# One k tile at a time: B of block 0 delivered in single k tiles between the row tiles of A, with 24 half-size staging slots

## The chip, the cores and the metric

The kernel runs on one core of one Trainium2 chip. The metric is the device time of one execution in microseconds (us). Executions of this kernel agree closely: 20 of the kernel before lie between 421.6 and 423.15 us. A difference of 1 us is therefore small but can be measured.

In the text PE is the matmul engine, DVE the vector engine, ACT the scalar engine, POOL the GpSimd engine and SP the sync engine. POOL and SP matter here mostly because they issue DMA transfers.

## The reference

```python
def setup_inputs():
    m, k, n = 1024, 4096, 4096
    return {"a": randn(m, k) as float32, "b": randn(k, n) as float32}   # shortened

def reference(a, b):
    x = np.matmul(a, b)
    return special.logsumexp(x, axis=-1).astype(np.float32)
```

A is 1024 x 4096, B is 4096 x 4096, and the output is one number for each of the 1024 rows.

## The kernel before

The kernel keeps A in SBUF as float16, transposed (`aT`), and goes through B in eight blocks of 512 columns. Blocks after the first use a scheme of sums and fewer products (its matmuls are on line 397 before and on line 416 after the change); it needs all of A transposed. This document is about the **opening**, in which A and block 0 of B arrive from HBM. Six of the eight row tiles of A are transposed by PE as they arrive, and their products with block 0 are done as plain matmuls in between.

A *round* of the opening is four k tiles (512 elements of k): six tiles of A, 128 x 512 each, and four k tiles of block 0 of B. There are eight rounds. A tile is 128 KB in float16, so a round writes 10 x 128 KB = 1.31 MB. POOL issues these transfers, because they cast float32 to float16 on the way. Only the first tile of A and the first two k tiles of B come as float32 from SP and are cast by DVE and ACT.

The order of arrivals, before. Two k tiles of B come in one transfer:

```python
    arrivals = []
    for k0 in range(0, KT, KN):            # KN = 4
        for m in range(MT - 2):            # six row tiles
            arrivals.append((k0, KN, "a", m))
            if m < KN // 2:
                arrivals.append((k0 + 2 * m, 2, "b", k0))
```

So a round is A0, B01, A1, B23, A2, A3, A4, A5: eight transfers. The work that follows an arrival, and the loading:

```python
    def behind(k0, kn, what, x):
        if what == "a":
            have_a.setdefault(k0, []).append(x)
            todo = [(k, x) for k in range(k0, k0 + kn) if k in have_b]
        else:
            have_b.update({k0: 1, k0 + 1: 1})
            todo = [(k, m) for k in (k0, k0 + 1) for m in have_a.get(x, [])]
        for k, m in todo:
            plain(acc[m // 2][m % 2], k // 2, k % 2, m)     # one 512-column matmul
        ...                                                 # (sums of A: cut)

    def first(k0, kn, what, x):
        ...                                                 # (A: cut, one SP transfer, DVE cast)
            raw = fix_pool.tile([P, 2, FD], f32, name="raw_b", tag="s")
            nc.sync.dma_start(out=raw, in_=b_rows[:, 0, :, 0:FD])
            nc.vector.tensor_copy(out=blk0.raw[0][:, 0, 0], in_=raw[:, 0])
            nc.scalar.copy(out=blk0.raw[0][:, 0, 1], in_=raw[:, 1])

    back = []
    for n, (k0, kn, what, x) in enumerate(arrivals):
        while coming and (coming[0][2] == "b" or loads[0] < count[0] + NSLOT):
            load(*coming.pop(0))            # POOL issues, as long as slots are free
            ...
        if what == "a":
            transpose_group(k0, kn, x)      # 4 PE transposes into PSUM, copy by DVE or ACT
        if k0 < KN and x < 3:
            warm(1)                         # a filler matmul
        if len(back) == 1 + (n >= MT) + (n >= 4 * MT):
            behind(*back.pop(0))            # matmuls lag the transposes by 1 to 3 arrivals
        back.append((k0, kn, what, x))
        while back and k0 < KN and what == "b":
            behind(*back.pop(0))
```

Of the kernel before, what the change touches and what calls it, by code (L numbers as in the profile page):

```python
# [13 lines left out]
def kernel(  # L14
# [6 lines left out]
    nc = tc.nc  # L21
    P = 128
    FD = 512
    H = FD // 2
    f32 = mybir.dt.float32
# [8 lines left out]
    MT, KT, NB = M // P, K // P, N // FD  # L34
    MP, KP = MT // 2, KT // 2
    G = 4
    GI = KP // G
    assert (MT, KT, NB) == (8, 32, 8)

    a_m = a.rearrange("(p mt) k -> mt p k", mt=MT)  # L40
    KN = 4
# [3 lines left out]
    fix_pool = ctx.enter_context(tc.tile_pool(name="fix", bufs=1))  # L45
# [12 lines left out]
            name=nc.get_next_instruction_name(),  # L58
# [8 lines left out]
    s2 = cst_pool.tile([P, KP, MP, P], f16, name="s2")  # L67
    s5 = cst_pool.tile([P, KP, MP, P], f16, name="s5")
    tb = cst_pool.tile([P, 3, KP, H], f16, name="tb")
    stg_slots = tb.rearrange("p t (i j) n -> p (t i) (j n)", j=4)  # L70
    NSLOT = 3 * KP // 4
    ident = cst_pool.tile([P, P], f16, name="ident")
    negmax = cst_pool.tile([P, MT, NB + 1], f32, name="negmax")
    tsum = cst_pool.tile([P, MT, NB + 1], f32, name="tsum")
# [50 lines left out]
    b_rows = b.rearrange("(i t p) n -> p i t n", p=P, t=2)  # L125

    class Block:
# [9 lines left out]
        def load(self, lo, hi):  # L137
            nc.gpsimd.dma_start(  # L138
                out=self.raw[lo // GI][:, lo % GI : lo % GI + hi - lo],
                in_=b_rows[:, lo:hi, :, ts(self.nb, FD)],  # L140
            )

        def load_all(self):
# [29 lines left out]
    blk0, blk1 = Block(0), Block(1)  # L173
# [13 lines left out]
    loads = [0]  # L187

    def load_a(k0, kn, m):
        slot = stg_slots[:, loads[0] % NSLOT, 0 : kn * P]  # L190
        loads[0] += 1
        nc.gpsimd.dma_start(out=slot, in_=a_m[m, :, k0 * P : (k0 + kn) * P])  # L192
        stg[k0, m] = slot

    count = [0]

    def transpose_group(k0, kn, m):
        src = stg.pop((k0, m))
        n = count[0]
        count[0] += 1  # L200
        pst = tps[n % 2]
        for j in range(kn):
            nc.tensor.matmul(  # L203
                pst[:, ts(j, P)],
                src[:, ts(j, P)],
                ident,
                is_transpose=True,
                start=(j == 0),
                stop=(j == kn - 1),
            )  # L210
        dst = aT[:, k0 // 2 : (k0 + kn) // 2, :, m // 2, m % 2, :]
        v = pst[:, 0 : kn * P].rearrange("p (i t c) -> p i t c", t=2, c=P)
        if n % 2 == 0:
            nc.vector.tensor_copy(out=dst, in_=v)  # L214
        else:
            nc.scalar.copy(out=dst, in_=v)  # L216
# [3 lines left out]
    def plain(pt, i, kp, m):  # L220
        nc.tensor.matmul(  # L221
            pt,
            aT[:, i, kp, m // 2, m % 2, :],
            blk0.raw[i // GI][:, i % GI, kp, :],
            start=(done[m] == 0),
            stop=(done[m] == KT - 1),
        )
        done[m] += 1

    def a_sums_early(r, q):  # L230
        a11, a12 = aT[:, r, 0, q, 0, :], aT[:, r, 1, q, 0, :]
        a21, a22 = aT[:, r, 0, q, 1, :], aT[:, r, 1, q, 1, :]
        add(s1[:, r, q], a11, a22)
        add(s2[:, r, q], a21, a22)
        add(s5[:, r, q], a11, a12)

    def a_sums_late(r, q):
        a11, a12 = aT[:, r, 0, q, 0, :], aT[:, r, 1, q, 0, :]
        a21, a22 = aT[:, r, 0, q, 1, :], aT[:, r, 1, q, 1, :]
        sub(a21, a21, a11)  # L240
        sub(a12, a12, a22)

    def first_max(m):
        lse_max(acc[m // 2][m % 2], m, 0)
        lse_exp(acc[m // 2][m % 2], m, 0)

    arrivals = []
    for k0 in range(0, KT, KN):
        for m in range(MT - 2):
            arrivals.append((k0, KN, "a", m))  # L250
            if m < KN // 2:
                arrivals.append((k0 + 2 * m, 2, "b", k0))
    in_place = []

    have_a, have_b = {}, {}

    def behind(k0, kn, what, x):
        if what == "a":
            have_a.setdefault(k0, []).append(x)
            todo = [(k, x) for k in range(k0, k0 + kn) if k in have_b]  # L260
        else:
            have_b.update({k0: 1, k0 + 1: 1})
            todo = [(k, m) for k in (k0, k0 + 1) for m in have_a.get(x, [])]
        for k, m in todo:
            plain(acc[m // 2][m % 2], k // 2, k % 2, m)
        r = slice(k0 // 2, (k0 + kn) // 2)
        if what == "a":
            if x >= 3 and in_place:
                a_sums_late(*in_place.pop(0))
            if x % 2 == 1 and k0 + kn < KT:  # L270
                a_sums_early(r, x // 2)
            if x == 5:
                in_place.extend([(r, 0), (r, 1), (r, 2)])
            if k0 + kn == KT and x == 4:
                first_max(0)
                first_max(1)
                for what in ("t1", "t6"):
                    blk1.make(what, 0, 2)

    def warm(n):  # L280
        for _ in range(n):
            nc.tensor.matmul(acc[2][1], zeros[:, 0:P], zeros[:, 0:FD], start=True, stop=True)  # L282

    zeros = s5[:, KP - 1].rearrange("p q c -> p (q c)")
    nc.vector.memset(zeros[:, 0:FD], 0.0)  # L285
    make_identity(nc, ident)
    nc.vector.memset(negmax, 3.0e38)
    nc.vector.memset(tsum, 0.0)
    warm(6)

    coming = list(arrivals)

    def first(k0, kn, what, x):
        if what == "a":
            raw = fix_pool.tile([P, FD], f32, name="raw_a", tag="e")
            slot = stg_slots[:, loads[0] % NSLOT, 0 : kn * P]
            loads[0] += 1
            nc.sync.dma_start(out=raw, in_=a_m[x, :, k0 * P : (k0 + kn) * P])
            nc.vector.tensor_copy(out=slot, in_=raw)
            stg[k0, x] = slot  # L300
        else:
            raw = fix_pool.tile([P, 2, FD], f32, name="raw_b", tag="s")
            nc.sync.dma_start(out=raw, in_=b_rows[:, 0, :, 0:FD])
            nc.vector.tensor_copy(out=blk0.raw[0][:, 0, 0], in_=raw[:, 0])
            nc.scalar.copy(out=blk0.raw[0][:, 0, 1], in_=raw[:, 1])

    def load(k0, kn, what, x):
        if len(coming) >= len(arrivals) - 2:
            first(k0, kn, what, x)
        elif what == "a":  # L310
            load_a(k0, kn, x)
        else:
            blk0.load(k0 // 2, k0 // 2 + 1)

    back = []
    for n, (k0, kn, what, x) in enumerate(arrivals):
        while coming and (coming[0][2] == "b" or loads[0] < count[0] + NSLOT):
            load(*coming.pop(0))
            if not coming:
                for lo in range(0, KP, 2):  # L320
                    blk1.load(lo, lo + 2)
        if what == "a":
            transpose_group(k0, kn, x)
        if k0 < KN and x < 3:
            warm(1)
        if len(back) == 1 + (n >= MT) + (n >= 4 * MT):
            behind(*back.pop(0))
        back.append((k0, kn, what, x))
        while back and k0 < KN and what == "b":
            behind(*back.pop(0))  # L330
    while back:
        behind(*back.pop(0))
    for m in range(2, MT - 2):
# [20 lines left out]
    for step, (_, qs) in enumerate(plan):  # L354
# [4 lines left out]
        if more:  # L359
            if plan[step + 1][0] is again1:  # L360
                nxt = last
            else:
                nxt = plan[step + 1][0]()
                if step == 1:
# [3 lines left out]
                        out=ident[0:1, 0:2], in_=aT[0:1, 0, 0, MP - 1, :, 0]  # L368
# [17 lines left out]
        for q in qs:  # L386
# [24 lines left out]
            s = fix_pool.tile([P, 4, H], f32, name=f"s_{step}_{q}", tag="s")  # L411
            x, e = s[:, 1::2], s[:, 0:2]
# [29 lines left out]
            if joint and q == 0:  # L442
                for lo in range(0, KP, 2):
# [9 lines left out]
                    for p in qs:  # L453
                        u0, u1 = quads[p]
                        k = (lo, lo + 2)
# [39 lines left out]
            if final:  # L495
# [13 lines left out]
                w = s.rearrange("p a n -> p (a n)")[:, 0 : H + 1]  # L509
# [14 lines left out]
                    out=w, in_=w, func=AF.Exp, bias=n0, scale=-1.0, accum_out=l0  # L524
# [81 lines left out]
```

## Time and profile before

| | before |
|---|---|
| time, median of the 6 runs first given | 422.01 us (421.8 to 422.56) |
| span of the profiled execution, first to last instruction | 419.5 us |
| PE busy | 412.3 us, 98% |
| first matmul of the later blocks (end of the opening) | 60.58 us |
| DMA from 12 to 50 us | 203 GB/s |

Two lines of the page of the kernel before: the busy times of the engines, and the chain of work that ended last, by engine.

```profile
PE 412.3 (98%) x3643; PEld 347.7 (83%) x3643; DVE 259.4 (62%) x575; ACT 109.7 (26%) x279; POOL 73.0 (17%) x113
PE 94%; DMA 4%; POOL 0%; issue 0%; ACT 0%; DVE 0%; POOLq 0%; ACTq 0%
```

PE is the limit of the whole, and the only other thing in the chain is DMA. The pieces of the chain in order of time, kernel before (start, length, what), show where that DMA part lies:

```profile
2.13 5.23 DMA b_0_83<-in_b_dram
...
8.35 6.28 DMA tb<-in_a_dram
15.16 6.76 DMA tb<-in_a_dram
```

All of it lies before 22 us. From there on the chain is PE alone, so what the opening gains or loses reaches the end. The list of PE's waits for the first 66 us, kernel before (engine, what it wrote, what it waited for: us in total, times, longest), says what there is to gain:

```profile
PE tps_97 L203 <- DMA tb<-in_a_dram: 0.9, 2, 0.6
```

PE stood 0.9 us for tiles of A. The same places in PE's timeline of the kernel before (start, length, engine, line, operation, out<-in, forms, count; in brackets the idle time before and its releaser):

```profile
4.27 0.61 PE L203 MATMUL tps_97<-ident,tb 128*128 128x128 f16 x4 [0.33 <-DVE tb L299]
5.73 0.60 PE L221 MATMUL acc_0_91<-b_0_83,aT 128*128 128x512 f16 x2 [0.38 <-DVE aT L214]
...
12.50 0.39 PE L203 MATMUL tps_97<-ident,tb 128*128 128x128 f16 x4
...
14.68 0.40 PE L203 MATMUL tps_97<-ident,tb 128*128 128x128 f16 x4 [0.27 <-DMA tb<-in_a_dram]
...
60.58 0.38 PE L397 MATMUL acc_0_0_763<-tb,s_71 128*128 128x256 f16 x2
```

The first plain matmuls run at 5.73 us, the seventh group of transposes (the second round) starts at 12.50, and the opening ends at 60.58. The windows of the kernel before (length, then for each engine its busy time and count; then granted clock, DMA share, GB/s) and POOL's timeline show the stream of transfers:

```profile
core 0: us, PE busy (x) PEld busy (x) DVE busy (x) ACT busy (x) POOL busy (x), PEclk, DMA share, GB/s
20.00:40.00 20.00, 19.38 (x143) 10.41 (x142) 12.10 (x52) 5.27 (x9) 13.71 (x25) 1.00 1.24 203
40.00:60.00 20.00, 20.00 (x145) 10.82 (x143) 14.24 (x58) 6.71 (x13) 14.48 (x23) 1.00 1.24 204
```

```profile
28.05 0.70 POOL L138 DMA_DIRECT2D b_2_85<-in_b_dram  x1 [0.54 <-DMA b_1_84<-in_b_dram]
28.90 1.83 POOL L192 DMA_DIRECT2D tb<-in_a_dram  x3
...
32.54 0.71 POOL L138 DMA_DIRECT2D b_2_85<-in_b_dram  x1 [0.23 <-DMA b_2_85<-in_b_dram]
```

An issue costs POOL about 0.53 us for a 128 KB tile and 0.70 us for a 256 KB pair. And POOL is not the limit: it waits, again and again, for an *earlier transfer* to complete. The order of issues and releases in the trace shows that an issue waits for the completion of the one eight issues earlier (the tenth, at 7.65 us, for the second, issued at 2.13), so eight are in flight. These waits, added up from 10 us to the last issue for A, come to 7.8 us.

### The profile page before, as it was taken

How to read it: one execution, taken by the hardware profiler on the slowest of the kernel's cores; microseconds unless marked ns; L12 is line 12 of the kernel's file. 1: busy time of each engine (PE TensorE's matmuls, PEld its weight loads, DVE VectorE, ACT ScalarE, POOL GpSimd, SP SyncE). 2: the span in 40 equal slices, each digit the busy share in tenths (PEclk: the TensorE clock that was granted, in tenths of full speed). 3: DMA queues.
4: the chain of work that ended last, by engine and by line, in shares of the span. 5: the costliest groups of instructions: out<-in, count | busy, mean ns of one | idle time of the engine just before them, and what ended most of it. 6: DMA issues, size and time to landing. Idle time of an engine off the chain costs nothing.

```text
span 419.5 us, 8526 instructions
## 1 busy us (share of the span) xinstructions
PE 412.3 (98%) x3643; PEld 347.7 (83%) x3643; DVE 259.4 (62%) x575; ACT 109.7 (26%) x279; POOL 73.0 (17%) x113
## 2 busy tenths in 40 slices
PE   7999999999999999999999999999999999999996
PEld 3555568888888888888888888888888888888885
DVE  2656587978656783258722694336832587299855
ACT  2222250141132222122222212222221222222124
POOL 8667753001010120003000030001200030020000
PEclk9999999999999999999999999999999999999999
DMA  9999999999999299003980079400990039899000
GB/s 185 203 203 203 203 206 206 207 207 215 176 202 197 43 191 207 5 2 47 207 149 2 2 124 207 74 2 2 188 207 8 2 55 207 141 183 208 13 2 1
DMA packets 57845, 53.37 MB, mean 127 GB/s; under 512 B 10192, under 2 KB 56912, under 8 KB 57808
## 3 DMA queue, kind: packets, MB, share of 16 engines
q0 software_dynamic: 48928, 49.95, 72.1%
q1 hardware_dynamic: 8880, 2.89, 4.1%
q8 instruction: 28, 0.46, 0.4%
q14 instruction: 9, 0.07, 0.0%
HBM read 100.66 MB, written 2.10 MB: 245 GB/s over the span
## 4 chain that ended last, share of the span: by engine, by line
PE 94%; DMA 4%; POOL 0%; issue 0%; ACT 0%; DVE 0%; POOLq 0%; ACTq 0%
DMA tb<-in_a_dram 3%; PE acc_1_0_1343 L397 2%; PE acc_1_0_765 L397 2%; PE acc_2_0_3103 L397 2%; PE acc_2_0_1478 L397 2%; PE acc_0_0_763 L397 2%; PE acc_3_0_2691 L397 2%; PE acc_0_0_2307 L397 2%; PE acc_1_0_1895 L397 2%; PE acc_3_0_4335 L397 2%; PE acc_2_0_4199 L397 2%; PE acc_0_0_3927 L397 2%; PE acc_3_0_3771 L397 2%; PE acc_2_0_3643 L397 2%; PE acc_3_0_2151 L397 2%; PE acc_0_0_1767 L397 2%
## 5 line engine op out<-in xcount | busy, mean ns | idle before, releaser
L397 PEld LDWEIGHTS <-aT 128*128 128x128 f16 x1856 | 181.6, 98 | 21.1
L397 PEld LDWEIGHTS <-s_71 128*128 128x128 f16 x464 | 45.4, 98 | 5.5
L397 PEld LDWEIGHTS <-s_72 128*128 128x128 f16 x464 | 45.4, 98 | 5.3
L397 PEld LDWEIGHTS <-s_73 128*128 128x128 f16 x464 | 45.4, 98 | 5.3
L221 PEld LDWEIGHTS <-aT 128*128 128x128 f16 x192 | 16.7, 98 | 13.6 <-DVE aT L214 1.2
L192 POOL DMA_DIRECT2D tb<-in_a_dram x47 | 25.5, 548 | 5.5 <-issue 2.1
L203 PEld LDWEIGHTS <-tb 128*128 128x128 f16 x192 | 13.9, 98 | 14.4 <-DMA tb<-in_a_dram 6.3
L216 ACT COPY aT<-tps_98 128x512 f16<-128x512 f16 x24 | 14.0, 585 | 38.3 <-PE tps_98 L203 38.3
L214 DVE COPY aT<-tps_97 128x512 f16<-128x512 f16 x24 | 10.2, 424 | 19.7 <-PE tps_97 L203 19.7
L84 DVE TENSOR_TENSOR aT<-aT 128x256 f16<-128x256 f16 (+1 forms) x56 | 16.1, 341 | 0.0
L203 PE MATMUL tps_97<-ident,tb 128*128 128x128 f16 x96 | 9.5, 223 | 1.2 <-DMA tb<-in_a_dram 0.9
L81 DVE TENSOR_TENSOR s_71<-aT 128x256 f16<-128x256 f16 (+1 forms) x26 | 8.2, 315 | 1.8 <-ACT aT L216 1.5
L203 PE MATMUL tps_98<-ident,tb 128*128 128x128 f16 x96 | 9.3, 219 | 0.0
L138 POOL DMA_DIRECT2D b_0_2299<-in_b_dram x1 | 0.9, 878 | 45.9 <-PE acc_3_0_2151 L397 45.9
L138 POOL DMA_DIRECT2D b_0_3379<-in_b_dram x1 | 0.9, 878 | 45.7 <-PE acc_3_0_3231 L397 45.7
L138 POOL DMA_DIRECT2D b_0_3919<-in_b_dram x1 | 0.9, 878 | 45.1 <-PE acc_3_0_3771 L397 45.1
L138 POOL DMA_DIRECT2D b_0_2839<-in_b_dram x1 | 0.9, 887 | 44.9 <-PE acc_3_0_2691 L397 44.9
L81 DVE TENSOR_TENSOR s_72<-aT 128x256 f16<-128x256 f16 (+1 forms) x26 | 8.2, 315 | 0.0
L81 DVE TENSOR_TENSOR s_73<-aT 128x256 f16<-128x256 f16 (+1 forms) x26 | 8.2, 315 | 0.0
L138 POOL DMA_DIRECT2D aT<-in_b_dram x4 | 3.5, 896 | 21.5 <-PE acc_1_0_4055 L397 21.5
L81 DVE TENSOR_TENSOR tb<-aT 128x1024 f16<-128x1024 f16 x8 | 5.2, 686 | 1.7 <-DMA aT<-in_b_dram 1.7
L282 PE MATMUL acc_1_96<-s_73 128*128 128x512 f16 x11 | 4.4, 524 | 1.2 <-DVE s_73 L285 1.2
(1050 smaller groups left out, 891.2 us busy)
## 6 DMA issues: line engine op xcount, KB each, us to landing
tb<-in_a_dram POOLq DMA_DIRECT2D x47, 128.0 KB, 5.9
aT<-in_b_dram POOLq DMA_DIRECT2D x4, 1024.0 KB, 15.3
b_1_84<-in_b_dram POOLq DMA_DIRECT2D x4, 256.0 KB, 6.6
b_2_85<-in_b_dram POOLq DMA_DIRECT2D x4, 256.0 KB, 6.2
b_3_86<-in_b_dram POOLq DMA_DIRECT2D x4, 256.0 KB, 6.2
b_0_87<-in_b_dram POOLq DMA_DIRECT2D x2, 512.0 KB, 8.6
b_1_88<-in_b_dram POOLq DMA_DIRECT2D x2, 512.0 KB, 11.8
b_2_89<-in_b_dram POOLq DMA_DIRECT2D x2, 512.0 KB, 15.2
```

What stands on the lines that cost most here:

```text
L81: nc.vector.tensor_tensor(out=o, in0=x, in1=y, op=ALU.add)
L84: nc.vector.tensor_tensor(out=o, in0=x, in1=y, op=ALU.subtract)
L138: nc.gpsimd.dma_start(out=self.raw[lo // GI][:, lo % GI : lo % GI + hi - lo], in_=b_rows[:, lo:hi, :, ts(self.nb, FD)],)
L192: nc.gpsimd.dma_start(out=slot, in_=a_m[m, :, k0 * P : (k0 + kn) * P])
L203: nc.tensor.matmul(pst[:, ts(j, P)], src[:, ts(j, P)], ident, is_transpose=True, start=(j == 0), stop=(j == kn - 1),)
L214: nc.vector.tensor_copy(out=dst, in_=v)
L216: nc.scalar.copy(out=dst, in_=v)
L221: nc.tensor.matmul(pt, aT[:, i, kp, m // 2, m % 2, :], blk0.raw[i // GI][:, i % GI, kp, :], start=(done[m] == 0), stop=(done[m] == KT - 1),)
L282: nc.tensor.matmul(acc[2][1], zeros[:, 0:P], zeros[:, 0:FD], start=True, stop=True)
L397: nc.tensor.matmul(c, lhs(i), rhs(i), start=(start and i == 0), stop=(i == KP - 1), skip_group_check=True,)
```

## The change

The intent: let each k tile of B arrive alone, A and B in turn, so that the third tile of A no longer stands behind four k tiles of B, and PE gets matmuls sooner and more evenly. Staging slots of half the size (24 instead of 12) allow more tiles of A ahead. The first pair of B is also split into two transfers from SP, and the identity matrix and two memsets are moved so that POOL's first transfer starts earlier. Core of the diff, with cuts marked:

```diff
-    stg_slots = tb.rearrange("p t (i j) n -> p (t i) (j n)", j=4)
-    NSLOT = 3 * KP // 4
+    stg_slots = tb.rearrange("p t (i j) n -> p (t i) (j n)", j=2)
+    NSLOT = 3 * KP // 2
 ...
+        def load_k(self, k):
+            i = k // 2
+            nc.gpsimd.dma_start(
+                out=self.raw[i // GI][:, i % GI, k % 2],
+                in_=b_rows[:, i, k % 2, ts(self.nb, FD)],
+            )
 ...
         for m in range(MT - 2):
-            arrivals.append((k0, KN, "a", m))
-            if m < KN // 2:
-                arrivals.append((k0 + 2 * m, 2, "b", k0))
+            arrivals.append((k0, "a", m))
+            if m < KN:
+                arrivals.append((k0, "b", k0 + m))
+    arrivals[2:8] = [(0, w, x) for w, x in (("b", 1), ("a", 1), ("b", 2), ("a", 2), ("b", 3), ("a", 3))]
 ...
-            have_b.update({k0: 1, k0 + 1: 1})
-            todo = [(k, m) for k in (k0, k0 + 1) for m in have_a.get(x, [])]
+            have_b[x] = 1
+            todo = [(x, m) for m in have_a.get(k0, [])]
 ...
-            raw = fix_pool.tile([P, 2, FD], f32, name="raw_b", tag="s")
-            nc.sync.dma_start(out=raw, in_=b_rows[:, 0, :, 0:FD])
 ...
+            if x == 0:
+                casts["raw"] = fix_pool.tile([P, 2, FD], f32, name="raw_b", tag="s")
+            raw = casts["raw"][:, x]
+            nc.sync.dma_start(out=raw, in_=b_rows[:, 0, x, 0:FD])
+            op = nc.vector.tensor_copy if x else nc.scalar.copy
+            casts[what, x] = lambda: op(out=blk0.raw[0][:, 0, x], in_=raw)
 ...                                  (identity after the 4th arrival, memsets after the 12th: cut)
+        if what == "a" and n < 6:
+            warm(2 if n < 5 else 1)
+        r = k0 // KN
+        if len(back) == 1 + (r > 0) + (r > 3):
             behind(*back.pop(0))
```

A round is now A0, B0, A1, B1, A2, B2, A3, B3, A4, A5: ten transfers of 128 KB, with the same bytes.

More of the change, by code (lines that the diff above doesn't have):

```diff
@@ L249, with behind @@
         for m in range(MT - 2):
-            arrivals.append((k0, KN, "a", m))
-            if m < KN // 2:
-                arrivals.append((k0 + 2 * m, 2, "b", k0))
+            arrivals.append((k0, "a", m))
+            if m < KN:
+                arrivals.append((k0, "b", k0 + m))
+    arrivals[2:8] = [(0, w, x) for w, x in (("b", 1), ("a", 1), ("b", 2), ("a", 2), ("b", 3), ("a", 3))]
     in_place = []
     have_a, have_b = {}, {}
-    def behind(k0, kn, what, x):
+    def behind(k0, what, x):
+        kn = KN
         if what == "a":
@@ L285, with first, load @@
     nc.vector.memset(zeros[:, 0:FD], 0.0)
-    make_identity(nc, ident)
-    nc.vector.memset(negmax, 3.0e38)
-    nc.vector.memset(tsum, 0.0)
     warm(6)
     coming = list(arrivals)
-    def first(k0, kn, what, x):
+    def first(k0, what, x):
         if what == "a":
             raw = fix_pool.tile([P, FD], f32, name="raw_a", tag="e")
-            slot = stg_slots[:, loads[0] % NSLOT, 0 : kn * P]
+            slot = stg_slots[:, loads[0] % NSLOT]
             loads[0] += 1
-            nc.sync.dma_start(out=raw, in_=a_m[x, :, k0 * P : (k0 + kn) * P])
-            nc.vector.tensor_copy(out=slot, in_=raw)
+            nc.sync.dma_start(out=raw, in_=a_m[x, :, k0 * P : (k0 + KN) * P])
+            casts[what, x] = lambda: nc.vector.tensor_copy(out=slot, in_=raw)
             stg[k0, x] = slot
         else:
-            raw = fix_pool.tile([P, 2, FD], f32, name="raw_b", tag="s")
-            nc.sync.dma_start(out=raw, in_=b_rows[:, 0, :, 0:FD])
-            nc.vector.tensor_copy(out=blk0.raw[0][:, 0, 0], in_=raw[:, 0])
-            nc.scalar.copy(out=blk0.raw[0][:, 0, 1], in_=raw[:, 1])
-    def load(k0, kn, what, x):
-        if len(coming) >= len(arrivals) - 2:
-            first(k0, kn, what, x)
+            if x == 0:
[4 more added lines that the diff above has]
+            casts[what, x] = lambda: op(out=blk0.raw[0][:, 0, x], in_=raw)
+    casts = {}
+    def load(k0, what, x):
+        n = len(arrivals) - len(coming)
+        if n <= 3:
+            first(k0, what, x)
         elif what == "a":
-            load_a(k0, kn, x)
+            load_a(k0, KN, x)
         else:
-            blk0.load(k0 // 2, k0 // 2 + 1)
+            blk0.load_k(x)
+        if n == 4:
+            make_identity(nc, ident)
+        if n == 12:
+            nc.gpsimd.memset(negmax, 3.0e38)
+            nc.gpsimd.memset(tsum, 0.0)
     back = []
-    for n, (k0, kn, what, x) in enumerate(arrivals):
-        while coming and (coming[0][2] == "b" or loads[0] < count[0] + NSLOT):
+    for n, (k0, what, x) in enumerate(arrivals):
+        while coming and (coming[0][1] == "b" or loads[0] < count[0] + NSLOT):
             load(*coming.pop(0))
@@ L321 @@
                     blk1.load(lo, lo + 2)
+        if n < 3:
+            casts[what, x]()
         if what == "a":
-            transpose_group(k0, kn, x)
-        if k0 < KN and x < 3:
-            warm(1)
-        if len(back) == 1 + (n >= MT) + (n >= 4 * MT):
+            transpose_group(k0, KN, x)
+        if what == "a" and n < 6:
+            warm(2 if n < 5 else 1)
+        r = k0 // KN
+        if len(back) == 1 + (r > 0) + (r > 3):
             behind(*back.pop(0))
-        back.append((k0, kn, what, x))
-        while back and k0 < KN and what == "b":
-            behind(*back.pop(0))
+        back.append((k0, what, x))
+        while back and r == 0 and what == "b":
+            behind(*back.pop())
     while back:
```

## The prediction

> **What bounds the kernel now.** The page gives PE 98% of the 419.5 us span; the chain of waits is 94% PE, 4% DMA. All of the DMA part lies before 21.96 us; after that the chain is PE alone. The change touches only the opening, up to the first L397 matmul at 60.58 us (PE timeline). From there PE runs without gaps to about 415.5 us, so what the opening gains or loses passes to the end. The opening holds 48 groups of four transposes (0.22 us each between starts) and 192 matmuls of 512 columns (0.216 us): 52.1 us. It starts at 4.27 us, so at best it ends at 56.4; some 4.2 us are gaps, including 5 filler matmuls (1.1 us). The list of PE waits names 0.9 us for tiles of A (at 14.68 and 21.96 us).
>
> DMA is nearly balanced with PE: the windows show 201 to 207 GB/s, so a round (six tiles of A, four k tiles of B, 1.31 MB) takes 6.45 us, against 6.5 us of PE.
>
> **What the change does.** Bytes are unchanged. In each round the third tile of A comes after two k tiles of B instead of four, 256 KB or 1.3 us earlier. Both DMA waits (0.9 us; 1.2 us with small gaps like them) should go. The first b tile splits, so the first plain matmul should start at about 5.2 us instead of 5.73; the first POOL DMA starts 0.7 us earlier.
>
> Added: 30 issues of B instead of 15 on POOL (0.55 us each against 0.70; POOL is about 80% busy there now), and a different PE order. In rounds two to four it becomes transposes of tile 1, one matmul, transposes of tile 2, then a matmul that reads tile 1. Between the start of tile 1's transposes and that matmul lie only 0.66 us of PE work, while the copy on ACT needs about 1.06 us (0.42 until it starts, 0.585 copy, 0.05 release). So PE waits 0.4 us in each of three rounds, 1.2 us. From the fifth round the backlog is three deep: no such wait. In the first round I expect waits of 0.4 to 0.6 us for the copies of tiles 1, 2 and 3.
>
> 24 half-size slots gain almost nothing: POOL waited for a slot 0.6 us in all. The Trainium skill ("DMA: Bandwidth & Descriptors", Anatomy of one DMA) gives about 2 us fixed cost per transfer; here 128 KB take 5.9 us to land (DMA issues), so queueing dominates and splitting should cost little bandwidth.
>
> A step-by-step estimate with these durations puts before's opening at 60.3 us (trace 60.6) and after's at 60.5 to 61.1. Waits for data are replaced by waits for copies.
>
> **Prediction.** 422.2 us, range 421.2 to 423.5. Faster by over 2%: 0.01; within 2%: 0.98; slower by over 2%: 0.01.
>
> **What would show it.** The first L397 matmul within 0.6 us of 60.6; PE waits for DMA of A nearly gone; new PE waits of about 0.4 us on ACT near 15, 22 and 29 us and on copies before 12 us; about 203 GB/s from 10 to 60 us; POOL near 95% busy there; the time from first L397 to the end unchanged within 0.2 us.
>
> **What would make it wrong.** If ten POOL issues a round take over 6.5 us (an issue plus the 0.17 us gap seen after waits is 0.72), DMA falls below 203 GB/s and the result is 1 to 3 us slower. If copies return sooner, PE runs without the 0.4 us waits and gains up to 1.3 us, bounded by the arrival of block 1 (its first sum waits for DMA at 58.9 us).

## The result, and the profile after

| | before | after |
|---|---|---|
| time, median, runs taken side by side | 422.23 us (421.6 to 423.15, 20 runs) | 425.88 us (424.71 to 427.21, 10 runs) |
| ratio after/before, 95% interval | | 1.0085 (1.0074 to 1.0096) |
| span of the profiled execution | 419.5 us | 425.0 us |
| first plain matmul / seventh group of transposes | 5.73 / 12.50 us | 5.91 / 17.43 us |
| end of the opening | 60.58 us | 65.18 us |
| from there to the end of the span | 358.9 us | 359.8 us |
| DMA from 12 to 50 us | 203 GB/s | 190 GB/s |

Ratios are computed as the mean time of one kernel's fast runs over that of the other's of the same rounds, so they are not quite the ratio of the medians. The change costs 3.65 us by the medians, 0.85%. That is within 2%, but outside the predicted range. The profiled execution of after is one of its longer ones (426.74 us), and that of before one of its shorter (421.73), so the span is 5.5 us longer; I take the *kinds* of loss from it and the *sizes* from timed runs.

The same two lines of the page of the kernel after:

```profile
PE 415.6 (98%) x3643; PEld 349.2 (82%) x3643; DVE 259.2 (61%) x573; ACT 109.8 (26%) x279; POOL 78.1 (18%) x130
PE 95%; DMA 1%; DVE 1%; ACT 1%; issue 0%; SPq 0%; DVEq 0%; ACTq 0%
```

The DMA part of the chain fell from 4% to 1%, as the change intended, and yet the kernel is slower. This is the trap: a smaller share of DMA in the chain is no gain in itself. The head of that chain, kernel after:

```profile
1.65 6.23 DMA raw_b<-in_b_dram
7.91 0.44 DVE b_0_83 L313
8.39 0.59 PE acc_0_91 L228
```

PE's waits in the first 66 us, kernel after:

```profile
PE acc_0_91 L228 <- DVE b_0_83 L313: 1.9, 1, 1.9
...
PE acc_1_92 L228 <- ACT aT L223: 0.7, 3, 0.2
```

PE's waits for tiles of A are gone. New is one wait of 1.9 us for a cast of B. PE's timeline of the kernel after, at the places shown before:

```profile
3.95 0.61 PE L210 MATMUL tps_97<-ident,tb 128*128 128x128 f16 x4
...
5.91 0.58 PE L228 MATMUL acc_0_91<-b_0_83,aT 128*128 128x512 f16 x1 [0.50 <-ACT b_0_83 L313]
8.39 0.59 PE L228 MATMUL acc_0_91<-b_0_83,aT 128*128 128x512 f16 x1 [1.89 <-DVE b_0_83 L313]
...
10.91 0.63 PE L228 MATMUL acc_0_91<-b_0_83,aT 128*128 128x512 f16 x1
11.33 0.63 PE L228 MATMUL acc_1_92<-b_0_83,aT 128*128 128x512 f16 x1
...
17.43 0.39 PE L210 MATMUL tps_97<-ident,tb 128*128 128x128 f16 x4
...
19.59 0.39 PE L228 MATMUL acc_1_92<-b_0_83,aT 128*128 128x512 f16 x1 [0.24 <-ACT aT L223]
...
65.18 0.38 PE L416 MATMUL acc_0_0_779<-tb,s_71 128*128 128x256 f16 x2
```

**First loss: the very beginning.** The second half of the first pair of B lands 2.7 us after the first (at 7.88 and 5.22 us). After that wait, matmuls of 512 columns start every 0.43 us (10.91, 11.33) instead of every 0.216, until about 13.3 us. By the seventh group of transposes the kernel is 4.93 us behind before (17.43 against 12.50). The half rate is what the Trainium skill ("TensorE: Matmul & The Clock Gate", Part 1: The HAM clock gate) describes: the array runs at half clock after it has stood idle, and at full clock after a few us of sustained work, with 426.7 and 215.7 ns from start to start for 512 columns. This trace agrees in the sizes (0.43 and 0.216 us). PE does not fall to that rate in the stop: in both kernels it runs at it from its first filler matmuls on, at 1.2 us (0.427 us from start to start). In before, the trace's record of the granted clock goes to full at 4.84 us; in after it does so only at 13.33. The half rate of the start lasts 8.5 us longer. The profile's row of granted clock does not tell it, since windows ahead of the first record read 1.00, as does the one from 10 to 20 us.

The first pair by its tile, before and then after (line, engine, operation, count, duration in ns, first and last start; then from issue to landing in us):

```profile
L303 SPq DMA_DIRECT2D raw_b<-in_b_dram x1: 414/414/414, 1.2 to 1.2; - x1
DMA to landing us min/median/max: 3.7/3.7/3.7
```

```profile
L311 SPq DMA_DIRECT2D raw_b<-in_b_dram x2: 416/420/424, 1.2 to 1.7; - x2
L313 DVE CAST b_0_83<-raw_b x1: 427/427/427, 7.9 to 7.9; 128x512 f16<-128x512 f32 x1
DMA to landing us min/median/max: 4.0/5.1/6.2
```

The half that is issued second, at 1.65 us, needs 6.2 us, for half the bytes. What runs against it is POOL's stream. The DMA queues in the stretch from 3.5 to 4.0 us, before and then after (queue: packets, MB, packet time as a share of 16 engines):

```profile
q1 hardware_dynamic: 98, 0.19, 100.1%
q0 software_dynamic: 1, 0.00, 1.2%
```

```profile
q0 software_dynamic: 43, 0.04, 58.9%
q1 hardware_dynamic: 19, 0.02, 17.9%
```

Queue q1 holds SP's transfers, q0 POOL's. Before, SP's are almost done (0.06 MB are left in the next half microsecond) when POOL's packets begin. After, q1 moved 0.18 and 0.13 MB in the two half microseconds ahead of this one; it falls to 0.02 MB once q0 is running, with SP's work unfinished, and recovers only slowly (0.05 and 0.09 MB in the next two). The Trainium skill ("DMA: Bandwidth & Descriptors", Queues, rings and completion order) says that each DMA engine takes turns between queues, packet by packet. A queue that comes second then loses rate; the trace agrees in direction, though a fall from 0.18 to 0.02 MB is much more than a half.

**Second loss: the stream.** The windows of the kernel after:

```profile
20.00:40.00 20.00, 19.52 (x144) 10.87 (x143) 12.30 (x54) 5.27 (x9) 14.67 (x29) 1.00 1.21 189
40.00:60.00 20.00, 20.00 (x151) 11.40 (x150) 13.27 (x55) 5.26 (x9) 16.02 (x29) 1.00 1.22 193
```

DMA falls from 203 and 204 to 189 and 193 GB/s. And POOL's timeline of the kernel after:

```profile
49.83 0.53 POOL L199 DMA_DIRECT2D tb<-in_a_dram  x1 [0.25 <-issue]
50.35 0.54 POOL L145 DMA_DIRECT2D b_3_86<-in_b_dram  x1
51.14 0.53 POOL L199 DMA_DIRECT2D tb<-in_a_dram  x1 [0.25 <-issue]
```

An issue of A and one of B, with the gap of 0.25 us before them, take 1.30 us (49.83 to 51.14). At 203 GB/s these 256 KB take 262,144 B / 203 GB/s = 1.29 us. The waits that the profile puts down to DMA, from 10 us to the last issue for A, are 2.68 us against 7.8 before.

It is tempting to read this as a POOL that can only just keep pace. The issues in the recorded traces say otherwise. Take each issue between 12 and 50 us, and subtract from its start the time at which the transfer eight issues earlier landed. In after, 42 of 55 issues start a fixed 0.28 or 0.53 us after that landing, also where the profile puts the gap down to "issue" (the three of A from 49.83 to 52.44: 0.53 us each). In before it is 42 of 46; in before_pool_busy (experiment 7), where POOL really is too busy, none of 36. So POOL in after still mostly waits for an earlier transfer; most of the other 13 come about 0.1 us later, right behind the issue ahead of them. As many transfers are in flight as before (7.4 on average, from issue to landing, in both), but they are smaller: 0.97 MB against 1.22. The longest waits (1.76 us at 7.97, 1.22 at 26.10, 1.11 at 55.38) are all for an earlier transfer too.

In this execution the first loss hides the slower stream: PE, almost 5 us late, found its tiles there. From the seventh group of transposes to the end of the opening, after took 47.75 us and before 48.08.

**A small third one.** From the end of the opening to the end of the span there are 0.9 us more. DVE's timeline at the border, before and then after:

```profile
62.33 0.75 DVE L81 TENSOR_TENSOR tb<-b_0_87 128x512 f16<-128x512 f16 x2
```

```profile
63.08 0.69 DVE L87 TENSOR_REDUCE negmax<-acc_0_91 128x1 f32<-128x512 f32 x1 [0.58 <-PE acc_0_91 L228]
...
67.75 0.75 DVE L81 TENSOR_TENSOR tb<-b_0_87 128x512 f16<-128x512 f16 x2
```

The last k tile of B now comes after the fourth tile of A, so the first two accumulators are complete only at about 63 us, 2 us before the border. DVE then takes all six maxima between 63.08 and 67.75, where in before only four fell at the border, and the sum that the second step of block 1 needs starts 2.6 us after the border (67.75 - 65.18) instead of 1.75 us (62.33 - 60.58). By the starts of its matmuls PE has three gaps there, 0.5 us together. The other 0.4 us lies after PE's last matmul: 4.39 us from its end to the end of the span, against 4.02 in before.

### The profile page after: what moved, and what is told of

Its sections match the earlier page's. It is cut to its first block, busy times and chain, and to the rows that moved or that the text cites. A ratio compares the mean times of both kernels' runs of the same rounds, so it can differ in the third digit from the quotient of the medians.

```text
span 425.0 us, 8535 instructions
## 1 busy us (share of the span) xinstructions
PE 415.6 (98%) x3643; PEld 349.2 (82%) x3643; DVE 259.2 (61%) x573; ACT 109.8 (26%) x279; POOL 78.1 (18%) x130
## 4 chain that ended last, share of the span: by engine, by line
PE 95%; DMA 1%; DVE 1%; ACT 1%; issue 0%; SPq 0%; DVEq 0%; ACTq 0%
PE acc_1_92 L228 2%; PE acc_1_0_1359 L416 2%; PE acc_0_93 L228 2%; PE acc_2_0_3659 L416 2%; PE acc_3_0_2167 L416 2%; PE acc_0_0_1783 L416 2%; PE acc_3_0_4487 L416 2%; PE acc_1_0_4071 L416 2%; PE acc_0_0_3403 L416 2%; PE acc_2_0_2579 L416 2%; PE acc_3_0_4351 L416 2%; PE acc_0_0_3943 L416 2%; PE acc_2_0_3119 L416 2%; PE acc_1_0_2991 L416 2%; PE acc_2_0_1494 L416 2%; PE acc_0_0_1227 L416 2%
## 5 line engine op out<-in xcount | busy, mean ns | idle before, releaser
L210 PEld LDWEIGHTS <-tb 128*128 128x128 f16 x192 | 15.1, 100 | 14.2 <-DMA tb<-in_a_dram 2.4
L291 PE MATMUL acc_1_96<-s_73 128*128 128x512 f16 x11 | 5.5, 632 | 1.2 <-DVE s_73 L294 1.2
L228 PE MATMUL acc_0_91<-b_0_83,aT 128*128 128x512 f16 x8 | 3.7, 462 | 2.4 <-DVE b_0_83 L313 1.9
```

The costliest lines, as they stand in the source:

```text
L210: nc.tensor.matmul(pst[:, ts(j, P)], src[:, ts(j, P)], ident, is_transpose=True, start=(j == 0), stop=(j == kn - 1),)
L228: nc.tensor.matmul(pt, aT[:, i, kp, m // 2, m % 2, :], blk0.raw[i // GI][:, i % GI, kp, :], start=(done[m] == 0), stop=(done[m] == KT - 1),)
L291: nc.tensor.matmul(acc[2][1], zeros[:, 0:P], zeros[:, 0:FD], start=True, stop=True)
```

## The experiments

Two theories, each an explanation of a part that could also have been the whole:

- **S**: splitting the first pair of B costs the time. The second half is overtaken by POOL's stream, PE stops, and it runs at half rate for longer.
- **R**: ten issues a round instead of eight cost the time. POOL has no slack, and the stream falls below what PE needs.
- Rivals to both: the new order of matmuls (waits for copies), the finer arrivals themselves, or the 24 slots.

### 1. one_raw_b: after, with the first pair in one transfer

```diff
-            nc.sync.dma_start(out=raw, in_=b_rows[:, 0, x, 0:FD])
+            if x == 0:
+                nc.sync.dma_start(out=casts["raw"], in_=b_rows[:, 0, :, 0:FD])
```

> The changed kernel, but the first two k tiles of B come in one 512 KB transfer on SP as before; all else stays (finer B, 24 slots, new order). Theory S (the split of the first pair is the loss: its second half landed at 7.9 us and PE waited and fell to half rate): the pair lands at about 4.9 us, no PE wait over 0.6 us before 12 us, first L416-type matmul at 60.5 to 61.5, time 421.5 to 423. Theory R (the finer stream is the loss: 30 issues on POOL lower the DMA rate): time stays 424.5 to 426.

Measured: 424.47 us (4 runs), ratio to before 1.0053 (1.0035 to 1.0071). The pair landed 3.6 us after issue, the stop of 1.9 us is gone, and the opening ended at 62.58 us. Between 20 and 60 us DMA ran at 190 and 193 GB/s, and PE waited 0.4 us for A. So about 1.4 us came back. S holds, but it isn't all: two microseconds of loss remain, with the stream still slow.

### 2. before_split: before, with the first pair split

```diff
-            nc.sync.dma_start(out=raw, in_=b_rows[:, 0, :, 0:FD])
+            for t in range(2):
+                nc.sync.dma_start(out=raw[:, t], in_=b_rows[:, 0, t, 0:FD])
```

> The kernel before, with only its first 512 KB transfer of B split in two 256 KB transfers on SP. Theory S: the second half lands 1 to 3 us later than 4.9 us, and the time rises to 423.5 to 426. Theory R: nothing changes, 421.8 to 422.6.

Measured: 424.33 us (4 runs), 1.0048 (1.0027 to 1.007), 1.7 us slower than before by the medians. PE's timeline of before_split:

```profile
5.25 0.61 PE L221 MATMUL acc<-b,aT 128*128 128x512 f16 x1
7.89 0.58 PE L221 MATMUL acc<-b,aT 128*128 128x512 f16 x1 [2.04 <-ACT b L306]
```

The halves landed 3.2 and 5.5 us after issue, PE stood 2.0 us, and it ran at half rate until 13.65 us, where the record of the granted clock goes to full (4.84 in before). The stream stayed at 203 GB/s. The split alone does all that the beginning of after shows, in a kernel whose order and stream are the old ones.

### 3. fill_warm: after, with eight filler matmuls in the stop

```diff
+        if n == 1:
+            warm(8)
```

> The changed kernel with 8 filler matmuls between the first and second plain matmul, where PE idles for b1. They add no data dependence. If half of the loss is the PE rate after the idle time (0.42 us a matmul from 8.4 to 12.9 us), the work after 8.4 us runs at 0.216 us and the time falls by about 2 us, to 423.5 to 424.5, although b1 lands no earlier. If the slow matmuls have another cause, the time stays 425.5 to 426.5.

Measured: 424.56 us (4 runs), 1.0052 (1.0035 to 1.0069). The second half still came late (5.7 us after issue). PE's timeline of fill_warm:

```profile
5.45 1.89 PE L291 MATMUL acc<-s 128*128 128x512 f16 x8
7.89 0.38 PE L228 MATMUL acc<-b,aT 128*128 128x512 f16 x1 [0.55 <-DVE b L313]
```

The plain matmul is still at 7.89 us, but PE ran at full rate from 4.71 us on (granted clock) and stayed there. Keeping PE busy with useless work saved 1.3 us against after (425.88 - 424.56), about as much as undoing the split did in one_raw_b (1.4). So of the first loss a large part is the half rate that goes with the stop, not the stop itself.

### 4. and 12. pool_late and pool_late_2: after, with POOL's first transfer held back

Both have the same edit: 24 memsets of two small tiles on POOL, ahead of its first transfer.

```diff
     coming = list(arrivals)
+    for _ in range(12):
+        nc.gpsimd.memset(negmax, 3.0e38)
+        nc.gpsimd.memset(tsum, 0.0)
```

> The changed kernel with 24 small memsets on POOL before its first DMA, which starts about 2 us later. If b1 is late because it shares the DMA engines with the POOL stream, b1 lands near 5 us instead of 7.9. If it is late because it is third in the SP queue or because small transfers are slow, it lands after 7 us still. Time: between 422.5 and 425 in the first case (later A tiles may cost some), 426 to 428 in the second.

> pool_late again, because its profile fell in one execution of 1123 us with PE slow throughout. In that one b0 and b1 landed 3.0 and 3.6 us after their issue. If that holds in a normal execution, b1 lands by 5.5 us and PE does not stop before 6 us; the time stays near 426 since the stream of A starts 2 us later.

Measured: the profile of pool_late fell in an execution of 1123.57 us, in which PE was slow throughout; it is set aside, and its cause is unknown. The three other runs gave 425.41 to 426.98 us (ratio 1.0087). So it was repeated for one look: 424.73 us (a single run, state unknown). There POOL's first transfer was issued at 3.30 us instead of 1.24, and the two halves landed 3.7 and 3.9 us after issue instead of 4.0 and 6.2. With POOL's stream out of the way the second half is as fast as the first: the late landing comes from the stream and not from there being two transfers. The time expected for this case, 422.5 to 425 us, was missed by the runs of pool_late: as a remedy it is useless, since the stream itself then starts 2 us later.

### 5. before_fine: before from the second round on with B in single k tiles, A and B in turn

```diff
-            if m < KN // 2:
+            if k0 == 0 and m < KN // 2:
                 arrivals.append((k0 + 2 * m, 2, "b", k0))
+            elif k0 > 0 and m < KN:
+                arrivals.append((k0 + m, 1, "b", k0))
 ...                                        (have_b and todo over kn tiles: cut)
-            blk0.load(k0 // 2, k0 // 2 + 1)
+            if kn == 2:
+                blk0.load(k0 // 2, k0 // 2 + 1)
+            else:
+                i = k0 // 2
+                nc.gpsimd.dma_start(out=blk0.raw[i // GI][:, i % GI, k0 % 2],
+                                    in_=b_rows[:, i, k0 % 2, 0:FD])
```

> The kernel before, with the finer arrival of B (one k tile per transfer, between the tiles of A) from the second round of four k tiles on; first round, 12 slots and all else as before. If the finer stream is a second loss of its own (theory R as a second term: one_raw_b stayed at 424.5 with 188 to 198 GB/s), the DMA rate from 20 to 60 us falls to 188 to 196 GB/s and the time is 423.8 to 425. If the rest of the loss of one_raw_b lies in the first round, it is 421.5 to 422.8.

Measured: 424.7 us (4 runs), 1.0054 (1.0022 to 1.0087), 2.3 us slower. The stream ran at 191 to 193 GB/s, PE waited 1.5 us for A and 0.4 us for B, and POOL's waits for DMA were 2.2 us. The beginning is that of before (first pair whole). So the finer stream costs time by itself, and here, where PE is not late, it shows as waits for DMA.

### 6. one_raw_coarse: after, with both undone, everything else kept

```diff
-            nc.sync.dma_start(out=raw, in_=b_rows[:, 0, x, 0:FD])
+            if x == 0:
+                nc.sync.dma_start(out=casts["raw"], in_=b_rows[:, 0, :, 0:FD])
 ...
-            if m < KN:
+            if k0 == 0 and m < KN:
                 arrivals.append((k0, "b", k0 + m))
+            elif k0 > 0 and m < KN // 2:
+                arrivals.append((k0, "b", k0 + 2 * m))
 ...
-            blk0.load_k(x)
+            blk0.load_k(x) if k0 == 0 else blk0.load(x // 2, x // 2 + 1)
```

> The changed kernel with the first pair of B in one transfer and, from the second round on, B in pairs of k tiles as before. Both suspected losses are undone, the rest of the change stays (24 slots, finer first round, new filler order, identity after the first POOL load). If the two terms are all of the loss: 421.5 to 422.8, DMA at 200 to 206 GB/s. If slots or order cost something of their own: above 423.3.

Measured: 422.06 us (4 runs), 0.9989 (0.9972 to 1.0006). The stream is back at 203 GB/s, and the opening ended at 61.23 us. The loss is gone. The 24 slots, the moved identity, the fillers and the order of the first round, which are all still there, neither cost nor gain anything that four runs resolve.

### 7. and 10. before_pool_busy and pool_light: before, with extra work on POOL

```diff
         nc.gpsimd.dma_start(out=slot, in_=a_m[m, :, k0 * P : (k0 + kn) * P])
+        if k0 > 0:                          # pool_light: if k0 > 0 and m in (1, 4)
+            for _ in range(2):              # pool_light: one memset
+                nc.gpsimd.memset(junk, 0.0)
```

> The kernel before, with two small memsets on POOL after each load of A from the second round on: POOL then has about 6.5 us of work a round, as the changed kernel has, but the transfers keep their sizes (eight in flight hold 1.31 MB instead of 1.05 MB). If POOL's time is what lowers the DMA rate, it falls below 198 GB/s and the time rises to 423.5 to 425. If it is the bytes in flight, the rate stays 200 to 206 and the time 421.8 to 422.8.

> The kernel before with two small memsets on POOL a round (after tiles 1 and 4), a seventh to a sixth of the load that before_pool_busy added: POOL then has about 5.8 to 6.2 us a round. If POOL costs nothing while it has slack, the rate stays 200 to 206 GB/s and the time 421.8 to 422.9. If each addition to POOL costs time in proportion (12 us for twelve memsets a round, so 2 us for two), it is 424 or more.

Measured: before_pool_busy 434.45 us (4 runs), 1.028 (1.0256 to 1.0305); DMA fell to 153 to 156 GB/s, and PE waited 11.3 us for A. POOL's timeline of before_pool_busy:

```profile
28.25 0.53 POOL L193 DMA_DIRECT2D tb<-in_a_dram  x1 [0.33 <-PE tps L207]
28.77 0.39 POOL L196 MEMSET junk<- 128x72 f32 x2
29.50 0.53 POOL L193 DMA_DIRECT2D tb<-in_a_dram  x1 [0.33 <-issue]
```

I had overshot: a load of A with its two memsets and gaps took 1.25 us (28.25 to 29.50), where the intended 6.5 us a round leave 0.85 us (6.5 less two pairs of 0.70, over six), and POOL never waited for DMA any more. It shows only that a POOL that is too busy does lower the rate of DMA, with the transfers themselves unchanged. pool_light, with two memsets a round in all, gave 422.2 us (4 runs), 0.9995 (0.9977 to 1.0012), and POOL's waits for DMA went from 7.8 to 6.35 us. In its profile DMA ran at 194 GB/s from 20 to 40 us, below the 200 to 206 expected, and at 203 from 40 to 60. So this much work on POOL costs no time that four runs resolve.

### 8. act_queue: after, with the second half issued from ACT's queue

```diff
-            nc.sync.dma_start(out=raw, in_=b_rows[:, 0, x, 0:FD])
+            (nc.scalar if x else nc.sync).dma_start(out=raw, in_=b_rows[:, 0, x, 0:FD])
```

The load of ACT's function table was moved behind that issue.

> The changed kernel with the second half of the first B pair issued from ACT's queue (before its table load) at about 0.75 us instead of third on SP at 1.65 us. If b1 was late because it was issued last and met the POOL stream, it lands by 5 us, PE does not stop, and the opening is that of one_raw_b: 424 to 425, with the finer stream as the remaining loss. If a separate 256 KB transfer is slow by itself, b1 lands after 6.5 us and the time stays above 425.3.

Measured: 424.36 us (4 runs), 1.004 (1.0019 to 1.0062). The second half, issued at 0.74 us, landed about 3.9 us later, and the stop is gone. But the first tile of A, issued at the same moment, took 4.0 us, and the first transposes started at 5.21 instead of 3.95 us, with PE at half rate until 9.70 us. Three transfers in one stretch share its rate: the delay moved from B to A.

### 9. pair_tail: after, whole first pair, with the last two tiles of A of a round in one transfer

```diff
-        elif what == "a":
+        elif what == "a" and k0 > 0 and x >= 4:
+            if x == 4:
+                load_pair(k0, x)            # one transfer into two neighbouring slots
+        elif what == "a":
             load_a(k0, KN, x)
```

> one_raw_b (424.5) with the last two row tiles of A of each round, from the second on, in one 256 KB transfer: nine issues on POOL a round instead of ten, B still one k tile at a time. If the finer stream loses because ten issues leave POOL no slack (6.5 us of POOL against 6.45 us of DMA a round), nine leave about 0.5 us: the DMA rate from 20 to 60 us rises from about 190 to 198 GB/s or more and the time falls to 422 to 423.4. If small B transfers are slow in the DMA engines themselves, the rate stays below 195 and the time at 424 to 425.

Measured: 424.11 us (4 runs), 1.0034 (1.0015 to 1.0053). Inconclusive: in its profiled execution the unsplit first pair took 5.1 us to land, so PE waited 1.6 us and ran at half rate until 10.28 us, which covers what was to be seen. The stream ran at 193 to 199 GB/s, between the two. It also shows that a whole pair can land late in this opening, in which POOL starts at 1.24 us.

### 11. pair_order: before, with the pairs of B one tile of A later

```diff
-            if m < KN // 2:
-                arrivals.append((k0 + 2 * m, 2, "b", k0))
+            j = m if k0 == 0 else m - 1
+            if 0 <= j < KN // 2:
+                arrivals.append((k0 + 2 * j, 2, "b", k0))
 ...
-        if len(back) == 1 + (n >= MT) + (n >= 4 * MT):
+        if len(back) == 1 + (n >= MT):
```

> A try to have the gain without the cost: the kernel before with B still in pairs, but from the second round on each pair one row tile later (a0 a1 b01 a2 b23 a3 a4 a5), and a backlog of two steps throughout. The third tile of A arrives 256 KB earlier with eight issues on POOL. An estimate with the measured durations puts the opening 0.3 to 1 us shorter than before: 421.3 to 422.0 if so; if the waits only move, 422.0 to 422.8.

Measured: 422.08 us (6 runs), 0.9992 (0.9978 to 1.0006). This was the attempt to have the intent of the change, no waits for A, at eight issues a round. In its trace PE has no wait for DMA at all, the stream ran at 203 GB/s, and the opening ended at 60.17 us, 0.4 us earlier than before. In the times that gain can't be told from nothing.

### 13. two_issues: before, with each pair of B as two issues, in the same order

```diff
-            blk0.load(k0 // 2, k0 // 2 + 1)
+            if k0 < KN:
+                blk0.load(k0 // 2, k0 // 2 + 1)
+            else:
+                i = k0 // 2
+                for t in range(2):
+                    nc.gpsimd.dma_start(out=blk0.raw[i // GI][:, i % GI, t],
+                                        in_=b_rows[:, i, t, 0:FD])
```

> The kernel before, with each pair of k tiles of B, from the second round on, issued as two 128 KB transfers one right after the other: ten POOL issues a round, but arrivals and PE order as before. If the number of issues is the cause: DMA 188 to 199 GB/s from 20 to 60 us, POOL waits for DMA down from 7.8 us to 2 to 4, time 423.8 to 425 as before_fine. If the order of arrivals and of PE work is the cause: 200 to 206 GB/s, 421.8 to 422.8.

Measured: 424.6 us (422.4, 424.74, 426.02, 424.45), 1.0061 (1.004 to 1.0083). Nothing but the number of issues has changed: order, matmuls, bytes and the beginning are those of before. It is as slow as before_fine. The waits that the profile puts down to DMA fell to 0.43 us, yet 39 of 58 issues start at the fixed distance from the landing of the eighth earlier transfer (see the second loss). The four times spread more than those of before, and the profiled execution is the fastest of them (422.4), so its stream of 200 to 202 GB/s is not that of the slow ones.

### 14. fine_a_pairs: before_fine, with the tiles of A in pairs

B comes in single k tiles, A in three pairs: seven issues a round.

```diff
-            elif k0 > 0 and m < KN:
-                arrivals.append((k0 + m, 1, "b", k0))
+            elif k0 > 0 and m in (1, 3):
+                arrivals.append((k0 + m - 1, 1, "b", k0))
+                arrivals.append((k0 + m, 1, "b", k0))
 ...
+        elif what == "a" and k0 > 0:
+            if x % 2 == 0:
+                load_pair(k0, x)
```

> before_fine (424.7) with A in pairs of row tiles, 256 KB a transfer, from the second round on: B still one k tile a transfer, seven POOL issues a round, 1.4 to 1.5 MB in flight. If POOL's issues (and the eight in flight) starve the DMA engines, the rate returns to 200 to 206 GB/s and the time to 421.8 to 423. If 128 KB transfers of B are slow in themselves, the rate stays under 197 and the time at 424 or more.

Measured: 422.19 us (4 runs), 0.9994 (0.9979 to 1.001). The windows of fine_a_pairs:

```profile
20.00:40.00 20.00, 19.39 (x146) 10.65 (x145) 12.87 (x54) 5.28 (x9) 12.86 (x21) 1.00 1.24 204
```

With B just as fine but fewer issues, the stream is back at 204 GB/s and the loss is gone. So single k tiles of B are not the cause; the count of issues (or what goes with it, see below) is.

### 15. after_again: the changed kernel once more

> The changed kernel once more, one look. If the late second half is a property of this program: b1 lands 5 us or more after its issue again, PE stops for over 1 us before the second plain matmul and runs at 0.42 us a matmul after it; time 424.7 to 427.2. If the first profile was an odd one, b1 lands within 4.2 us.

Measured: 425.46 us (one run, state unknown). The second half landed 5.5 us after issue, PE stood 2.06 us, and here the granted clock was full from 5.13 us, half from 8.54 and full again from 11.96 (0.90 in the row, from 10 to 20 us). The stream ran at 200 GB/s, and the opening ended at 63.90 us. So the late half and the time at half rate belong to the kernel and not to one execution: in one the full rate came late, in the other it was lost again. The rate of the stream varies from one execution to another; why was not found.

### What the runs add up to

| kernel | first pair | issues a round | median us | ratio to before of the same rounds |
|---|---|---|---|---|
| before | whole | 8 | 422.23 | 1 |
| one_raw_coarse | whole | 8 | 422.06 | 0.9989 |
| fine_a_pairs | whole | 7 | 422.19 | 0.9994 |
| before_split | split | 8 | 424.33 | 1.0048 |
| one_raw_b | whole | 10 | 424.47 | 1.0053 |
| before_fine | whole | 10 | 424.7 | 1.0054 |
| two_issues | whole | 10 | 424.6 | 1.0061 |
| after | split | 10 | 425.88 | 1.0085 |

Each of the two costs about 2 us alone (1.7 for the split; 1.9 in one_raw_b and 2.3 in before_fine and two_issues for ten issues, by the medians of their own rounds). Together they cost 3.65, against a sum of 3.6 to 4.0; the runs do not resolve a difference. None of the kernels beats before clearly.

**What stays open.** With smaller transfers and eight in flight, fewer bytes are in flight as well (at most 8 x 128 KB = 1.05 MB after, a whole round of 1.31 MB before; 0.97 and 1.22 MB on average). two_issues and fine_a_pairs change POOL's time per round and the bytes in flight at once, and pair_tail did not decide. before_pool_busy shows that POOL's time alone can lower the rate. But the starts of the issues (second loss) speak for the other: with ten issues a round, most still wait for the transfer eight issues earlier (42 of 55 in after, 40 of 55 in one_raw_b, 39 of 58 in two_issues, 33 of 56 in before_fine), and POOL's own time holds up only the rest, by about 0.1 us each. So the times show that more and smaller transfers are the cause; the way in which they cost is argued from traces. Bytes in flight are not the whole account either, since the stream ran at 201 GB/s in the profile of two_issues and at 192 in that of before_fine, both with 0.96 MB in flight. Also open are the run of 1123.57 us, and why the first pair, unsplit, landed late in the profile of pair_tail and not in that of one_raw_b.

## Why the prediction was wrong

- **"PE 98% ... what the opening gains or loses passes to the end": right.** The opening ended 4.60 us later and the span grew by 5.5.
- **"Both DMA waits (0.9 us ...) should go": right.** In the list of waits of after, none for a tile of A is left.
- **"PE waits 0.4 us in each of three rounds": right, in cause and place.** By the starts of the matmuls, 0.41 us are lost before 19.59 (the transposes of 18.96 take 0.22), and the same before 26.52 and 33.45; the profile puts 0.24 us of each down as a wait. In the first round 0.45 us were lost at 15.47.
- **"The first b tile splits, so the first plain matmul should start at about 5.2 us": the first step that failed.** One plain matmul did start early in after_again (5.20 us), and at 5.91 in the first profile. But the prediction took the second half to land soon after the first. It was issued at 1.65 us, just as POOL's stream was about to start, landed 5.5 to 6.2 us later, and PE stood 2 us and then ran at half rate for 3.4 us (after_again) to 4.9 us (after). Measured alone (before_split): 1.7 us. I had seen only the gain in "the first POOL DMA starts 0.7 us earlier", and not what that transfer collides with. (It started 0.2 us earlier: 1.24 instead of 1.44.)
- **"Queueing dominates and splitting should cost little bandwidth", and a step-by-step estimate with a stream at full rate: the second step that failed.** The cost of an issue was read rightly, 0.55 us. Added up, it should have warned: 10 issues and their gaps are 6.5 us, equal to the 6.45 us that the bytes need. What the runs showed in place of "little": 190 GB/s instead of 203 in the profile of after, and 2.3 us lost when only the pairs of B are issued as two (two_issues). The prediction did name this under "what would make it wrong", with 1 to 3 us, which is the size found, and put it down to POOL's time; the fault was to leave it out of the middle of the range. By the starts of the issues, the smaller transfers in flight explain more of it than POOL's time does; which share each has stays open. The fixed cost of 2 us that I cited from the Trainium skill did not settle it: no run here measures that cost.
- **"POOL near 95% busy": wrong.** It was busy 29.1 of the 38 us from 12 to 50 (77%; before 70%, not the 80% read there); most of the gaps between are waits for an earlier transfer. **"About 203 GB/s": wrong**, 190.
- **"The time from first L397 to the end unchanged within 0.2 us": wrong**, 0.9 us longer: 0.5 us in PE's gaps at the border, where the first accumulators finish later and their maxima delay a sum of block 1, and 0.4 us after the last matmul.
- **"24 half-size slots gain almost nothing": right** (one_raw_coarse keeps them: 0.9989).

## What to carry to other kernels

Before a transfer is split, ask two things. Does the issuing engine's time for a round still fit into the time of the bytes (here ten issues of 0.53 us, against 6.45 us)? And how many transfers are kept in flight: here eight at most, so halving some took the bytes in flight from 1.22 to 0.97 MB. A transfer that PE needs at once should be finished before another queue starts streaming, or be one transfer issued first; being overtaken cost more here than its own delay, since PE then ran on at half rate. A gap that the profile puts down to "issue" may still be a wait: compare its end with the landings. Lower waits for DMA in the list are no proof of a gain: look at the time of the first work that both kernels share.

## What the Trainium skill lacked or had wrong

- "DMA: Bandwidth & Descriptors", Issuing engines are not separate DMA queues, says that the time to initiate a DMA is "usually small relative to the DMA itself", and the page gives no figure, by size, for how long one holds POOL. Here an issue holds it 0.53 us for 128 KB and 0.70 us for 256 KB. The bytes of a 128 KB tile take 0.645 us at 203 GB/s: the two are of nearly the same size.
- The same page, Queues, rings and completion order, says that engines take turns between queues by the packet, but not how unequally. Here the queue of SP fell from 0.13 MB in the half microsecond from 3.0 us to 0.02 MB in the next, when POOL's began, and the half pair issued second took 6.2 us to land, the first 4.0.
- "TensorE: Matmul & The Clock Gate", Part 1, puts the fall to half rate after an idle window of about 3.4 us, and does not say how much work keeps a window from counting as idle. The length agrees: in after_again the granted clock changes at 5.13, 8.54 and 11.96 us, 3.41 us apart both times. But the fall at 8.54 came though PE had worked for about 1.1 us since 5.13 (by its matmuls) and had stood for no more than about 2.2 us at a time.
